# A five-layer float32 kernel on one core: loads issued before their use, and another order of steps in the latent layer

## The chip, the core and the metric

The kernel runs on one core of a Trainium2 chip. A core has TensorE (PE, matrix products and transposes), VectorE (DVE), ScalarE (ACT), GpSimd (POOL) and SyncE (SP, whose queue issues every load and store here). The metric is the device time of one execution in microseconds (us), lower is better; it is given as the median of several runs.

## The reference, cut to what matters

Two blocks of float32 layers work on 256 tokens of 2048 features. The first has a retention layer and a dilated attention layer, each with attention to 256 memory tokens; the second has a sliding-window layer (SWA) over the tokens and 256 context tokens, and a latent attention layer (MLA). Two facts matter below. Scales and shifts come from a small vector through a large matrix (`ada`):

```python
shift, scale, gate = jnp.split(cond @ ada_w[i] + ada_b[i], 3, axis=-1)
h = rmsnorm_2(x, norm_g[i]) * (1.0 + scale) + shift
```

And the latent layer normalises its keys before 16 heads attend:

```python
kv = (rmsnorm_2(c_kv, kva_g) @ w_kvb).reshape(B, S, H, MLA_NOPE + MLA_V)
k_nope = rmsnorm_2(kv[..., :MLA_NOPE], kn_nope_g)
s = (einsum('bqhd,bkhd->bhqk', qn, kn) + einsum('bqhr,bkr->bhqk', qp, kp)) * scale
p = softmax(s); o = einsum('bhqk,bkhd->bqhd', p, v)
```

## The kernel before

**Products.** Nearly all time goes into products of 256 or 512 tokens with weights. `gemm` (L191) walks over the weights in units of 1 MB: `wload` (L127) loads a unit into one of four `raw` tiles, ScalarE rounds it to the fast product type (`wh`, L134, three tiles), VectorE makes the remainder (`wl`, L135, two tiles), and TensorE forms activation high times `wh`, activation low times `wh`, and activation high times `wl`. Results add up in `acc`, of which there are five PSUM banks; `add_halves` (L300, L301) empties four banks into `mkT` pages: ScalarE copies one half, VectorE adds the other.

**Side work.** After each unit `gemm` calls `tick`, which moves every running generator (`spawn`, `later`) by one `yield`, and `fill(nfill)`, which takes a unit of `ada` from a list when its credit passes 1. An ada unit is a 1 MB load through the same four `raw` tiles and eight VectorE instructions (L383, L385); there are 96 of them. FA, FB and FS are the credits for one unit in the first, second and SWA part. 66 pages of 128x512 hold everything else. A scheduler then sets each engine's order by the order of the program and by what is free, so the order on an engine is near the written one but not the same.

**The places that the change touches.** (1) `mem_rows` and `enter_x` (L605, L616), run beside the memory keys (`mem_kv`, L629): they load `nat` (rows, summed in squares by ScalarE, `junk`) and `natT` pages (the transposed input, split into `ha`), and use each at once. (2) `enter_ctx` (L905), the same for the context, beside the out-product of the dilated layer. (3) The entry of SWA: the sums of L944 to L962 give `r23`, then `hT_mod` scales (`y`, L895) and transposes (`yT`) the input for the first product `kr` (L1019), whose first two units are taken for the context half before that (`ahead=2`). (4) `reload` (L1052): eight pages of attention results that were stored to DRAM (`mixsd`) come back as `mixSL` and are split by ScalarE into `mixSH` and by VectorE into `mixSL` (L325, L326), for SWA's out-product. (5) The latent layer: its first product (L1250), `kv_T` and `cq_T` (transposes of the latents), and then per pair of heads `mla_q` (L1336), `mla_kv` (L1382) and `mla_att` (L1408). A chain (two blocks of queries by two heads make four) has three stages: scores `ls` and softmax `lp`; transposes `pT` copied to `pTs`; products `lo` with the values and a gated write to `mixl`. `pipe` starts one chain in each of its steps and yields after every second step (MPER).

Of the kernel before, what the change touches and what calls it, by code (L numbers as in the profile page):

```python
# [22 lines left out]
S128 = 128 ** -0.5  # L23
NPAGES = 66
NRAW = 4
FA, FB, FS = 0.25, 0.23, 0.58
NMISC = 3
MPER = 2


class Act:
# [29 lines left out]
def tile_kernel(ctx: ExitStack, tc: tile.TileContext, d, out):  # L61
# [17 lines left out]
    def pg(s="pg", dt=F32, shape=None):  # L79
        return ppool.tile(shape or [P, 512], dt, name=nm(s), tag="pg")  # L80
# [506 lines left out]
        for k in range(2):  # L587
            split_gain(act, 2 * i + k, u[:, k * 256 : (k + 1) * 256], gain(gi, 2 * i + k))

    def enter(srcT, act, gi, c):  # L590
        for i in (2 * c, 2 * c + 1):
            enter_page(srcT, act, gi, i)

    def rows(src, q, c):
        for t in range(2):
            u = pg("nat")
            load(u, src[t * P : (t + 1) * P, c * 512 : (c + 1) * 512])
            sumsq(q[:, 4 * t + c : 4 * t + c + 1], u, 512)

    def row_rsqrt(dst, q):  # L600
        ssq = small(2)
# [2 lines left out]

    def mem_rows():  # L605
        q = const([P, 8], "ssm")
        for c in range(4):
            rows(d["mem"], q, c)
            yield
        row_rsqrt(memr, q)  # L610
        condition()
        yield
        bcast_rows(memrB[:, 0:256], memr)
        yield from enter_x()

    def enter_x():  # L616
        q = const([P, 8], "ssxa")
        for c in range(4):
            enter(d["xT"], ha, N_A, c)
            rows(d["x"], q, c)  # L620
            yield
        row_rsqrt(ra, q)
        V.tensor_scalar(sra, ra, 1.0 / 16.0, None, ALU.mult)
        V.tensor_scalar(hra, ra, 0.5, None, ALU.mult)
# [3 lines left out]
    def mem_kv(layer):  # L628
        kT, vn = [None] * 4, [[None] * 2 for _ in range(2)]  # L629
        w = d["w_mem_kv"][layer]  # L630
        if layer == 1:
            accs = gemm_wide(hm, w, 1024, [(0, 1), (1, 1)] + [(u, 2) for u in range(2, NK, 2)],
                             lambda u: u % 2 == 0 and enter_page(d["memT"], hm, MEM_N, u // 2))
            spawn(mem_rows())
            vs = [[pg("mkv") for _ in range(2)] for _ in range(2)]
            for c in range(2):
                for t in range(2):
                    A.copy(vs[c][t], accs[c][t])

            def post():  # L640
                for c in range(2):
                    for t in range(2):
                        A.activation(vs[c][t], vs[c][t], AF.Copy, scale=memr[:, t : t + 1])
                        load(memb[4 + 2 * t + c], vs[c][t])
            later(post, 7)
        for c in range(2):
            raw = add_halves(gemm_HL(hm, w, c * 512, FA if layer == 0 or c else 0), "mkT")

            def post(c=c, raw=raw):
                for j in range(2):  # L650
                    V.tensor_tensor(raw[j].rearrange("p (k n) -> p k n", k=2), raw[j].rearrange("p (k n) -> p k n", k=2),
                                    bc(memrB[:, 0:256], 2), ALU.mult)
                    if layer == 1:
                        load(memb[2 * c + j], raw[j])
                    else:
                        kT[2 * c + j] = split_page(raw[j], "mkTs")
            later(post, 5 if layer == 1 and c == 0 else 0)
        if layer == 0:
            for c in range(2):
                acs = gemm(hm, [0, 1], w, NK, 1024 + c * 512, nfill=FA)  # L660
                for t in range(2):
                    vn[t][c] = split_rows(acs[t], memr[:, t : t + 1])
        return kT, vn
# [240 lines left out]

    def enter_ctx():  # L905
        q, rc = const([P, 8], "ssc"), const([P, 2], "rc")
        for c in range(4):
            rows(d["ctx_2"], q, c)
        row_rsqrt(rc, q)
        yield  # L910
        rcB = pg("rcB")
        bcast_rows(rcB[:, 0:256], rc)
        for i in range(8):
            u = pg("natT")
            load(u, d["ctxT"][i])
            V.tensor_tensor(u.rearrange("p (k n) -> p k n", k=2), u.rearrange("p (k n) -> p k n", k=2),
                            bc(rcB[:, 0:256], 2), ALU.mult)
            split_mod(hs, 2 * i, 2, u, modA[0][:, 1, 2 * i : 2 * i + 2], adaT[0][:, 2 * i : 2 * i + 2, 1])
            if i % 2:
                yield  # L920

    def splitB(u):
        if u == 12:
# [88 lines left out]
    def evac4(acs):  # L1012
        res = [None] * 4
        for i, t in enumerate(TL):
# [1 line left out]
            A.copy(res[t], acs[i])  # L1016
        return res

    kr = evac4(gemm(hs, TL, WS, NK, 2048, nfill=FS,  # L1019
                    pre=lambda u: hT_mod([z[0][u // 4], z[1][u // 4]], r23, 0, 0, hs, u // 4), ahead=2))  # L1020
    kn = [None] * 4
    for t in TL:
# [27 lines left out]
            mixS.H[k], mixS.L[k] = pg("mixSH", F32R), pg("mixSL", F32R)  # L1050

    def reload():  # L1052
        for u in range(0, 8, 4):
            for k in range(u, u + 4):
                open_page(k)
                q = mixS.L[k].bitcast(F32)
                load(q, mixsd[k])
                split_in_place(mixS, k)
            yield

    for j in range(4):
        qr = evac4(gemm(hs, TL, WS, NK, j * 512, nfill=FS))
# [171 lines left out]
    def rope_pe(dst, src, rs, t, o, g):  # L1234
# [11 lines left out]
        for j in range(2):  # L1246
# [1 line left out]
        V.tensor_tensor(dst, dst, b, ALU.add)  # L1248

    acs = gemm(None, [(hl[1], 0), (hl[1], 1), (hl[0], 0), (hl[0], 1)], WL, NK, 512, 320,  # L1250
               pre=lambda u: hT_mod([x3[0][u // 4], x3[1][u // 4]], r3, 1, 0, hl[0], u // 4))
    ckv, kpq = [None] * 4, [None] * 4
    for i, t in enumerate(TL):
        ss, u, rs = small(2), small(2), small(2)
# [27 lines left out]
                tr(ps[:, t * P : (t + 1) * P], kpq[t][:, o : o + P])  # L1282
            A.copy(dst, ps)

    later(kv_T)
    acs = gemm(hl[0], [0, 1], WL, NK, 0, 512)
    cq = []
    for t in range(2):
# [14 lines left out]
            for k in range(2):  # L1303
                split_gain(hq, 2 * j + k, ps[:, k * 256 : (k + 1) * 256], gT[:, 6 * NK + 2 * j + k : 6 * NK + 2 * j + k + 1])

    later(cq_T)
    mixl = new_act(NK, 256, "mixl")
    S192 = 192 ** -0.5
    gsl = {}
# [19 lines left out]
    def mla_q(hp, r):  # L1329
        acs = gemm(hq, [0, 1], d["mla_w_qb_2"], 4, hp * 384, 384, mid=True)  # L1330
        qn = [pg("qn") for _ in range(2)]
        qp = [pg("qp", F32R) for _ in range(2)]
        ss8, rs8, evs = small(8), small(8), []
        for t in range(2):
            ev = pg("qev")
            A.copy(ev[:, 0:384], acs[t][:, 0:384])  # L1336
            v4 = ev[:, 0:384].rearrange("p (e w) -> p e w", e=2)
            sq = pg("sq")
            A.activation(sq[:, 0:384], ev[:, 0:384], AF.Square)
            s4 = sq[:, 0:384].rearrange("p (e w) -> p e w", e=2)  # L1340
            V.tensor_reduce(ss8[:, 2 * t : 2 * t + 2], s4[:, :, 0:P], AX, ALU.add)
            V.tensor_reduce(ss8[:, 4 + 2 * t : 6 + 2 * t], s4[:, :, P:192], AX, ALU.add)
            evs.append((ev, sq))
        V.tensor_scalar(ss8[:, 0:4], ss8[:, 0:4], 1.0 / P, EPS, ALU.mult, ALU.add)
        V.tensor_scalar(ss8[:, 4:8], ss8[:, 4:8], 1.0 / 64, EPS, ALU.mult, ALU.add)
        G.tensor_tensor(rs8, ss8, nhalf[:, :8], ALU.pow)

        def scale(t):
            ev, sq = evs[t]
            v4 = ev[:, 0:384].rearrange("p (e w) -> p e w", e=2)  # L1350
            pe = sq[:, 384:512].rearrange("p (e w) -> p e w", e=2)
            q3 = qp[t][:, 0:256].rearrange("p (e s w) -> p e s w", e=2, s=2)
            for e in range(2):
                V.scalar_tensor_tensor(qn[t][:, e * P : (e + 1) * P], v4[:, e, 0:P], rs8[:, 2 * t + e : 2 * t + e + 1],
                                       g_qk, ALU.mult, ALU.mult)
            rope_q(pe, v4[:, :, P:192], rs8[:, 4 + 2 * t : 6 + 2 * t], t)
            V.tensor_copy(q3[:, :, 0, :], pe)
            V.tensor_tensor(q3[:, :, 1, :], pe, q3[:, :, 0, :].bitcast(F32), ALU.subtract)

        def post():  # L1360
            for t in range(2):
                scale(t)
            for _ in range(2):
                yield
            ps = misc("qT")
            for e in range(2):
                for t in range(2):
                    tr(ps[:, e * 256 + t * P : e * 256 + (t + 1) * P], qn[t][:, e * P : (e + 1) * P])
            r["q"] = split_page(ps, "qT")
            ps = misc("qpT")  # L1370
            for e in range(2):
                for t in range(2):
                    tr(ps[:, e * 256 + t * P : e * 256 + (t + 1) * P], qp[t].bitcast(F32)[:, e * P : (e + 1) * P])
            r["qp"] = pg("qpT", F32R)
            A.copy(r["qp"], ps)
        spawn(post())

    def mla_kv(hp, r):
# [13 lines left out]
        rsqrt(rs8, ss8, P)  # L1392

        def post():
            for t in range(4):
                v4 = kv[t].rearrange("p (e s w) -> p e s w", e=2, s=2)
                for e in range(2):
                    A.activation(v4[:, e, 0, :], v4[:, e, 0, :], AF.Copy, scale=rs8[:, 2 * t + e : 2 * t + e + 1])
            for _ in range(2):
                yield  # L1400
            r["k"] = []
# [7 lines left out]
    def mla_att(hp, r):  # L1409
# [34 lines left out]
            return [st0, st1, st2]  # L1444

        def attend():
            for _ in range(4):
                yield
            yield from pipe([chain(t, e) for t in range(2) for e in range(2)], MPER)
            mix_out(mix, mixl, hp)  # L1450

        spawn(attend())
# [116 lines left out]
```

## Time and profile before

| | us |
|---|---|
| median of 3 runs | 3096.49 (3095.86 to 3096.86) |
| the profiled execution | 3096.07 |
| its span, first to last instruction | 3094.3 |
| TensorE / VectorE / ScalarE / GpSimd busy | 3042.5 / 2163.8 / 1411.2 / 86.2 |
| mean granted TensorE clock, share of full speed | 0.995 |

The span is what the trace covers; 1.8 us of the execution's time lie around it. TensorE is busy 98% of the span, so the views to read are those of its waits and of the clock granted to it; a row of waits names the instruction that waited, and the one that released it.

### The profile page before, as it was taken

To read this page: it belongs to the slowest core of one execution; us is meant where nothing else is said; L and a number is where in the kernel's file an instruction comes from. 1 tells how busy PE (TensorE), PEld (TensorE's weight loads), DVE (VectorE), ACT (ScalarE), POOL (GpSimd) and SP (SyncE) were. 2 spreads that over 40 slices of the span, in tenths; PEclk is the share of its full clock that TensorE was granted. 3 is DMA by queue.
4 is the path that set the end of the run, shared out by engine and by line. 5 is a ranking of instruction groups with operands and counts; after the bars stand their busy time and mean duration, and the time that the engine had idled before them with its cause. 6 is when DMAs were issued, how large, how long until landed. Compare 5 with 4: busy or idle time off the path is not lost.

```text
span 3094.3 us, 38864 instructions
## 1 busy us (share of the span) xinstructions
PE 3042.5 (98%) x15386; PEld 2570.2 (83%) x15386; DVE 2163.8 (70%) x3277; ACT 1411.2 (46%) x1870; POOL 86.2 (3%) x63
## 2 busy tenths in 40 slices
PE   9799999999999999999999999999999999999999
PEld 7688888888888888888888888788888778888887
DVE  5677877878867767766766747867676766656774
ACT  6444444445433433433433555424355342645662
POOL 0000000000000000000000000010110100000110
PEclk9899999999999999999999999999999999999999
DMA  8776676677566656656656667544433435453234
GB/s 307 242 243 226 210 245 222 221 260 264 206 208 234 232 185 227 222 195 227 231 191 227 222 224 248 181 157 156 136 118 108 163 103 180 145 176 123 69 103 129
DMA packets 307863, 600.77 MB, mean 194 GB/s; under 512 B 12896, under 2 KB 24800, under 8 KB 307680
## 3 DMA queue, kind: packets, MB, share of 16 engines
q1 hardware_dynamic: 307680, 598.29, 57.3%
q8 instruction: 120, 1.97, 0.3%
q14 instruction: 63, 0.52, 0.0%
HBM read 585.62 MB, written 12.62 MB: 193 GB/s over the span
## 4 chain that ended last, share of the span: by engine, by line
PE 92%; DVE 4%; DMA 1%; ACT 1%; POOL 1%; issue 1%; SPq 0%; DVEq 0%; ACTq 0%
PE acc L99 83%; PE pT L111 2%; PE so L99 1%; PE bs L99 1%; PE ls L99 1%; PE bo L99 1%; DMA raw<-in_ada_w 1%; DVE wl L135 1%; PE xs L99 1%; DVE ada L385 1%; PE lo L99 1%; PE mixT L111 0%; PE mo L99 0%; PE ms L99 0%; PE yT L111 0%
## 5 line engine op out<-in xcount | busy, mean ns | idle before, releaser
L135 DVE TENSOR_TENSOR wl<-raw,wh 128x2048 fp32r<-128x2048 f32 (+2 forms) x437 | 982.2, 2248 | 601.8 <-PE acc L99 343.4
L134 ACT CAST wh<-raw 128x2048 fp32r<-128x2048 f32 (+2 forms) x437 | 821.0, 1879 | 1136.3 <-PE acc L99 1021.0
L385 DVE SCALAR_TENSOR_TENSOR ada<-raw,condth,ada 128x512 f32<-128x512 f32 x720 | 496.0, 745 | 60.7 <-DMA raw<-in_ada_w 60.5
L99 PE MATMUL acc<-hb,wh 128*128 128x512 f32 x896 | 232.6, 393 | 0.0
L99 PE MATMUL acc<-wh,ha 128*128 128x512 f32 x896 | 215.2, 392 | 0.0
L99 PE MATMUL acc<-hk,wh 128*128 128x512 f32 x768 | 199.4, 394 | 0.1
L99 PEld LDWEIGHTS acc<-wh,ha 128*128 128x128 f32 x896 | 166.3, 188 | 33.5
L99 PE MATMUL acc<-wh,hk 128*128 128x512 f32 x768 | 185.3, 393 | 0.0
L99 PEld LDWEIGHTS acc<-hb,wh 128*128 128x128 f32 x896 | 159.8, 188 | 27.0 <-DVE hb L443 0.5
L99 PEld LDWEIGHTS acc<-wh,hk 128*128 128x128 f32 x768 | 143.1, 188 | 28.6
L99 PEld LDWEIGHTS acc<-hk,wh 128*128 128x128 f32 x768 | 136.7, 188 | 22.5 <-DVE bq L301 0.4
L99 PE MATMUL acc<-wh,hsH 128*128 128x512 f32 x384 | 151.2, 397 | 0.0
L99 PE MATMUL acc<-wh,hsL 128*128 128x512 f32 x384 | 150.6, 395 | 0.0
L99 PEld LDWEIGHTS acc<-hb,wl 128*128 128x128 f32 x896 | 126.1, 190 | 11.8 <-ACT hb L442 0.2
L99 PE MATMUL acc<-hb,wl 128*128 128x256 f32 x896 | 129.8, 282 | 0.0
L99 PEld LDWEIGHTS acc<-hk,wl 128*128 128x128 f32 x768 | 108.0, 190 | 10.2
L99 PE MATMUL acc<-hk,wl 128*128 128x256 f32 x768 | 110.9, 282 | 0.0
L99 PE MATMUL acc<-wl,ha 128*128 128x512 f32 x448 | 110.7, 389 | 0.0
L99 PE MATMUL acc<-wh,mixSH 128*128 128x512 f32 x256 | 101.2, 400 | 5.8 <-ACT mixSH L325 3.8
L99 PE MATMUL acc<-wh,mixSL 128*128 128x512 f32 x256 | 101.0, 400 | 2.2 <-DVE mixSL L326 2.2
L99 PE MATMUL acc<-hsH,wh 128*128 128x512 f32 x256 | 99.7, 391 | 0.0
L99 PE MATMUL acc<-hsL,wh 128*128 128x512 f32 x256 | 99.3, 390 | 0.0
(404 smaller groups left out, 5405.1 us busy)
## 6 DMA issues: line engine op xcount, KB each, us to landing
raw<-in_ada_w SPq DMA_DIRECT2D x96, 1024.0 KB, 5.1
raw<-in_w_kv SPq DMA_DIRECT2D x96, 1024.0 KB, 5.0
raw<-in_w_in_b SPq DMA_DIRECT2D x80, 1024.0 KB, 5.0
raw<-in_w_in_a SPq DMA_DIRECT2D x64, 1024.0 KB, 5.3
raw<-in_swa_w_in SPq DMA_DIRECT2D x40, 1024.0 KB, 5.0
raw<-in_w_mem_kv SPq DMA_DIRECT2D x31, 1024.0 KB, 5.3
raw<-in_w_out_a SPq DMA_DIRECT2D x24, 1024.0 KB, 5.2
raw<-in_w_out_b SPq DMA_DIRECT2D x24, 1024.0 KB, 5.2
```

What stands on the lines that cost most here:

```text
L99: T.matmul(o, lhsT=l, rhs=r, start=start, stop=stop)
L111: T.transpose(o, i, ident[:k, :k])
L134: A.copy(h, rw)
L135: V.tensor_tensor(l, rw, h.bitcast(F32), ALU.subtract)
L385: V.scalar_tensor_tensor(a[ci], raw[:, k, :], col, a[ci], ALU.mult, ALU.add)
```

## The change

What it does, part by part. A helper `staged(n, begin, end, lag)` issues the loads of step i and uses those of step i-lag, one step a tick. `mem_rows` and `enter_x` run by it with a lag of 2, `enter_ctx` with a lag of 1 for rows and 2 for pages (one page a tick, before two), `reload` with two steps of four pages and a lag of 1. The `later` waits in `mem_kv` go from 7 to 8 and from 5 and 0 to 6 and 3. The `kr` product has no `nfill` (its four units give no ada credit), and FS goes from 0.58 to 0.64, so 44 units give 28.2 credits where 48 gave 27.8. The first product of the latent layer gets `ahead=2`. `kv_T` and `cq_T` come one tick later. The keys are scaled by 32 VectorE products of 128x2x128 in place of 64 ScalarE instructions of 128x128. `mla_q` and `mla_kv` yield once ahead of their scaling. `attend` waits five ticks in place of four and runs pairs of chains (the two heads of one block), one stage a tick, older pairs first.

```diff
-FA, FB, FS = 0.25, 0.23, 0.58
+FA, FB, FS = 0.25, 0.23, 0.64
-MPER = 2
...
+    def staged(n, begin, end, lag=2):
+        got = []
+        for i in range(n + lag):
+            if i < n:
+                got.append(begin(i))
+            if i >= lag:
+                end(i - lag, got[i - lag])
+            yield
...
     def mem_rows():
         q = const([P, 8], "ssm")
-        for c in range(4):
-            rows(d["mem"], q, c)
-            yield
+        yield from staged(4, lambda c: load_rows(d["mem"], c), lambda c, us: sum_rows(q, c, us))
...
     def enter_x():
-        for c in range(4):
-            enter(d["xT"], ha, N_A, c)
-            rows(d["x"], q, c)
-            yield
+        def begin(c):
+            return [load_page(d["xT"][i]) for i in (2 * c, 2 * c + 1)], load_rows(d["x"], c)
+        def end(c, got):
+            for i in range(2):
+                for k in range(2):
+                    split_gain(ha, 4 * c + 2 * i + k, got[0][i][:, k * 256 : (k + 1) * 256], gain(N_A, 4 * c + 2 * i + k))
+            sum_rows(q, c, got[1])
+        yield from staged(4, begin, end)
...
-            later(post, 7)
+            later(post, 8)
...
-            later(post, 5 if layer == 1 and c == 0 else 0)
+            later(post, (6, 3)[c] if layer == 1 else 0)
...
     def enter_ctx():
-        for c in range(4):
-            rows(d["ctx_2"], q, c)
+        yield from staged(4, lambda c: load_rows(d["ctx_2"], c), lambda c, us: sum_rows(q, c, us), 1)
...
+        yield from staged(8, lambda i: load_page(d["ctxT"][i]), end)
...
-    kr = evac4(gemm(hs, TL, WS, NK, 2048, nfill=FS,
+    kr = evac4(gemm(hs, TL, WS, NK, 2048,
                     pre=lambda u: hT_mod([z[0][u // 4], z[1][u // 4]], r23, 0, 0, hs, u // 4), ahead=2))
...
     def reload():
-        for u in range(0, 8, 4):
-            for k in range(u, u + 4):
+        def begin(i):
+            for k in range(4 * i, 4 * i + 4):
                 open_page(k)
-                q = mixS.L[k].bitcast(F32)
-                load(q, mixsd[k])
+                load(mixS.L[k].bitcast(F32), mixsd[k])
+        def end(i, _):
+            for k in range(4 * i, 4 * i + 4):
                 split_in_place(mixS, k)
-            yield
+        yield from staged(2, begin, end, 1)
...
-               pre=lambda u: hT_mod([x3[0][u // 4], x3[1][u // 4]], r3, 1, 0, hl[0], u // 4))
+               pre=lambda u: hT_mod([x3[0][u // 4], x3[1][u // 4]], r3, 1, 0, hl[0], u // 4), ahead=2)
...
-    later(kv_T)
+    later(kv_T, 1)
...
-    later(cq_T)
+    later(cq_T, 1)
...
         def post():
+            yield
             for t in range(2):
                 scale(t)
...
         def post():
+            yield
             for t in range(4):
-                v4 = kv[t].rearrange("p (e s w) -> p e s w", e=2, s=2)
-                for e in range(2):
-                    A.activation(v4[:, e, 0, :], v4[:, e, 0, :], AF.Copy, scale=rs8[:, 2 * t + e : 2 * t + e + 1])
+                k3 = kv[t].rearrange("p (e s w) -> p e s w", e=2, s=2)[:, :, 0, :]
+                V.tensor_tensor(k3, k3, rs8[:, 2 * t : 2 * t + 2].unsqueeze(2).to_broadcast([P, 2, P]), ALU.mult)
...
         def attend():
-            for _ in range(4):
+            for _ in range(5):
                 yield
-            yield from pipe([chain(t, e) for t in range(2) for e in range(2)], MPER)
+            pairs = [[chain(t, e) for e in range(2)] for t in range(2)]
+            for i in range(len(pairs) + 2):
+                for j in (2, 1, 0):
+                    if 0 <= i - j < len(pairs):
+                        for c in pairs[i - j]:
+                            c[j]()
+                yield
             mix_out(mix, mixl, hp)
```

Three places show how it moves instructions. Rows of the changed kernel carry its own line numbers. The first place is ScalarE beside the memory keys: `ha` and `junk` wait for loads of x, `mkT` empties the four PSUM banks of a finished product, `wh` prepares weights. Before:

```order
L123 ACTIVATE junk_815,ssxa<-nat_813 128x512
L123 ACTIVATE junk_819,ssxa<-nat_817 128x512
L319 ACTIVATE ha_129<-natT_859,gT 128x256
L319 ACTIVATE ha_130<-natT_859,gT 128x256
L319 ACTIVATE ha_131<-natT_865,gT 128x256
L319 ACTIVATE ha_132<-natT_865,gT 128x256
L300 COPY mkT_899<-acc_645 128x256
L300 COPY mkT_899<-acc_646 128x256
L300 COPY mkT_904<-acc_647 128x256
L300 COPY mkT_904<-acc_648 128x256
```

After, from the copy that ends the row scales `memrB`:

```order
L133 CAST wh_966<-raw_965 128x2048
L571 COPY memrB_137<-rB_815 128x256
L299 COPY mkT_839<-acc_637 128x256
L299 COPY mkT_839<-acc_638 128x256
L299 COPY mkT_844<-acc_639 128x256
L299 COPY mkT_844<-acc_640 128x256
L122 ACTIVATE junk_961,ssxa<-nat_823 128x512
L122 ACTIVATE junk_963,ssxa<-nat_824 128x512
L122 ACTIVATE junk_1019,ssxa<-nat_895 128x512
L133 CAST wh_1028<-raw_1027 128x2048
```

The copies of `mkT` stood behind six pages of `ha` and four of `junk`; they now stand ahead of all of them.

The second is SP at the end of SWA's last heads, where `mixSL` pages come back and `raw` carries weights and ada units. Before:

```order
L96 DMA raw_19593<-in_ada_w 128x4x512
L96 DMA mixSL_18981<-mixsd 128x512
L96 DMA mixSL_18986<-mixsd 128x512
L96 DMA raw_19603<-in_swa_w_out 128x4x512
L96 DMA mixSL_18991<-mixsd 128x512
L96 DMA raw_19765<-in_ada_w 128x4x512
L96 DMA mixSL_18996<-mixsd 128x512
L96 DMA raw_19828<-in_swa_w_out 128x4x512
L96 DMA mixSL_19055<-mixsd 128x512
L96 DMA raw_19914<-in_swa_w_out 128x4x512
```

After:

```order
L95 DMA raw_19593<-in_ada_w 128x4x512
L95 DMA mixSL_18967<-mixsd 128x512
L95 DMA mixSL_18970<-mixsd 128x512
L95 DMA mixSL_18973<-mixsd 128x512
L95 DMA mixSL_18976<-mixsd 128x512
L95 DMA mixSL_19033<-mixsd 128x512
L95 DMA mixSL_19036<-mixsd 128x512
L95 DMA mixSL_19039<-mixsd 128x512
L95 DMA mixSL_19042<-mixsd 128x512
L95 DMA raw_19603<-in_swa_w_out 128x4x512
```

The eight pages stood between five `raw` loads; they now follow one another behind a single one.

The third is TensorE in the latent attention, from the end of one chain's scores; `acc<-wl` rows belong to the product that runs beside it. Before:

```order
L99 MATMUL ls_22692<-kpHH_21285,qpT_22264 128x512
L99 MATMUL ls_22692<-kpLL_21286,qpT_22264 128x512
L111 MATMUL pT_22706<-ident,lp_22647 128x128 x4
L99 MATMUL lo_22713<-kv_22418,pTs_22658 128x128
L99 MATMUL lo_22713<-kv_22420,pTs_22658 128x128
L99 MATMUL lo_22713<-kv_22422,pTs_22658 128x128
L99 MATMUL lo_22713<-kv_22424,pTs_22658 128x128
L99 MATMUL acc_22769<-wl_22773,hkvH_21281 128x512
L99 MATMUL acc_22767<-wl_22773,hkvH_21282 128x512
L99 MATMUL ls_22719<-kT_22543,qT_22255 128x512
L99 MATMUL ls_22719<-kT_22543,qT_22256 128x512
L99 MATMUL ls_22719<-kT_22544,qT_22255 128x512
```

After:

```order
L98 MATMUL ls_22734<-kpHH_21285,qpT_22283 128x512
L98 MATMUL ls_22734<-kpLL_21286,qpT_22283 128x512
L98 MATMUL acc_22694<-wl_22700,hkvH_21281 128x512
L98 MATMUL acc_22695<-wl_22700,hkvH_21281 128x512
L98 MATMUL ls_22748<-kT_22543,qT_22274 128x512
L98 MATMUL ls_22748<-kT_22543,qT_22275 128x512
L98 MATMUL ls_22748<-kT_22544,qT_22274 128x512
L98 MATMUL ls_22748<-kpHH_21285,qpT_22283 128x512
L98 MATMUL ls_22748<-kpLL_21286,qpT_22283 128x512
L98 MATMUL acc_22696<-wl_22700,hkvH_21281 128x512
L98 MATMUL acc_22697<-wl_22700,hkvH_21281 128x512
L98 MATMUL acc_22694<-wl_22700,hkvH_21282 128x512
```

The transposes `pT` and products `lo` of the pair before stood right behind the scores; now the scores of both heads come first with eight rows of the running product around them (the last three are cut here), and `lo` and `pT` behind these.

On PE, SP and GpSimd the instructions are otherwise the same ones in number. VectorE has 32 scalings more and 15 copies of `pTs` fewer; ScalarE has 64 scalings fewer and these 15 copies more. At the entry of the latent layer the order on TensorE is the same in both kernels.

## Rows read from the trace of the kernel before

**Rows 1.** The page: busy us of an engine, share, instructions.

```profile
PE 3042.5 (98%) x15386; PEld 2570.2 (83%) x15386; DVE 2163.8 (70%) x3277; ACT 1411.2 (46%) x1870; POOL 86.2 (3%) x63
```

**Rows 2.** Waits of TensorE, whole span: total us, times, longest.

```profile
PE acc L99 <- DVE mkT L301: 16.6, 1, 16.6
PE acc L99 <- ACT wh L134: 7.1, 1, 7.1
PE acc L99 <- ACT mixSH L325: 3.8, 1, 3.8
PE yT L111 <- ACT y L895: 3.7, 2, 3.4
PE pT L111 <- ACT qpT L1375: 3.6, 3, 1.6
PE acc L99 <- DVE mixSL L326: 2.2, 2, 1.4
PE acc L99 <- ACT mixSH L316: 1.8, 1, 1.8
PE mixT L111 <- DVE mixl L1442: 1.2, 3, 0.7
PE acc L99 <- DVE hlH L339: 1.1, 1, 1.1
PE rB L99 <- DVE dg L569: 1.0, 1, 1.0
...
PE kvT L111 <- ACT ckv L1261: 0.7, 1, 0.7
...
PE kpT L111 <- DVE kpq L1265: 0.6, 1, 0.6
```

**Rows 3.** Busy time by window; the clock column (after POOL) is 0.50 throughout.

```profile
106.16:123.23 17.07, 4.75 (x14) 4.00 (x15) 7.27 (x17) 9.40 (x26) 0.00 (x0) 0.50 0.70 236
1939.12:1942.53 3.41, 2.88 (x11) 2.59 (x12) 2.83 (x6) 1.75 (x4) 0.00 (x0) 0.50 0.57 216
2461.36:2468.19 6.83, 5.34 (x12) 3.74 (x13) 6.83 (x14) 2.38 (x7) 0.00 (x0) 0.50 0.04 16
```

**Rows 4.** Timeline at 100 us: start, length, instruction, [idle before it <- releaser].

```profile
100.83 1.09 PE L99 MATMUL acc<-hm,wh 128*128 128x512 f32 x4
...
95.29 0.38 SPq L96 DMA_DIRECT2D raw<-in_ada_w  x1
...
112.63 0.91 ACT L319 ACTIVATE ha<-natT,gT 128x256 fp32r<-128x256 f32 x2 [4.07 <-DMA natT<-in_xT]
...
117.39 1.16 ACT L300 COPY mkT<-acc 128x256 f32<-128x256 f32 x4
...
101.28 5.38 DVE L385 SCALAR_TENSOR_TENSOR ada<-raw,condth,ada 128x512 f32<-128x512 f32 x8
...
117.92 1.41 DVE L301 TENSOR_TENSOR mkT<-acc,mkT 128x256 f32<-128x256 f32 x4
119.25 1.28 DVE L651 TENSOR_TENSOR mkT<-mkT,memrB 128x512 f32<-128x512 f32 x2
```

**Rows 5.** Timeline of VectorE ahead of the entry of SWA.

```profile
1924.60 3.40 DVE L385 SCALAR_TENSOR_TENSOR ada<-raw,condth,ada 128x512 f32<-128x512 f32 x5 [2.56 <-DMA raw<-in_ada_w]
...
1931.92 2.07 DVE L385 SCALAR_TENSOR_TENSOR ada<-raw,condth,ada 128x512 f32<-128x512 f32 x3
```

**Rows 6.** The key scaling (L1398): its time each, and what ScalarE awaited before it.

```profile
L1398 ACT ACTIVATE kv<-kv,sm x64: 385/392/406, 2809.4 to 2993.2; 128x128 f32<-128x128 f32 x64
...
  POOL sm L119: 13.4, 8
```

**Rows 7.** Groups by form: a VectorE product of 128x256, and the copies of pTs.

```profile
L301 DVE TENSOR_TENSOR bk<-acc,bk 128x256 f32<-128x256 f32 x48 | 20.0, 420 | 11.8 <-ACT bk L300 11.8
...
L499 DVE COPY pTs<-pT x27: 670/681/693, 1088.0 to 3015.8; 128x512 f32<-128x512 f32 x27
```

**Rows 8.** Busy time in the latent attention, columns as in rows 3.

```profile
2900.00:2950.00 50.00, 46.91 (x285) 40.05 (x285) 39.13 (x128) 34.24 (x79) 9.56 (x4) 1.00 0.22 74
```

More of the change, by code (lines that the diff above doesn't have):

```diff
@@ L588, in enter_page, with load_rows, sum_rows, load_page @@
             split_gain(act, 2 * i + k, u[:, k * 256 : (k + 1) * 256], gain(gi, 2 * i + k))
[L590 to L594, printed above, removed]
-        for t in range(2):
-            u = pg("nat")
-            load(u, src[t * P : (t + 1) * P, c * 512 : (c + 1) * 512])
-            sumsq(q[:, 4 * t + c : 4 * t + c + 1], u, 512)
+    def staged(n, begin, end, lag=2):
[6 more added lines that the diff above has]
+            yield
+    def load_rows(src, c):
+        us = [pg("nat") for _ in range(2)]
+        for t in range(2):
+            load(us[t], src[t * P : (t + 1) * P, c * 512 : (c + 1) * 512])
+        return us
+    def sum_rows(q, c, us):
+        for t in range(2):
+            sumsq(q[:, 4 * t + c : 4 * t + c + 1], us[t], 512)
+    def load_page(src):
+        u = pg("natT")
+        load(u, src)
+        return u
     def row_rsqrt(dst, q):
@@ L912, in enter_ctx, with end @@
         bcast_rows(rcB[:, 0:256], rc)
-        for i in range(8):
-            u = pg("natT")
-            load(u, d["ctxT"][i])
+        def end(i, u):
             V.tensor_tensor(u.rearrange("p (k n) -> p k n", k=2), u.rearrange("p (k n) -> p k n", k=2),
@@ L918, in enter_ctx @@
             split_mod(hs, 2 * i, 2, u, modA[0][:, 1, 2 * i : 2 * i + 2], adaT[0][:, 2 * i : 2 * i + 2, 1])
-            if i % 2:
-                yield
+        yield from staged(8, lambda i: load_page(d["ctxT"][i]), end)
     def splitB(u):
@@ L1052, in reload @@
     def reload():
-        for u in range(0, 8, 4):
-            for k in range(u, u + 4):
+        def begin(i):
+            for k in range(4 * i, 4 * i + 4):
                 open_page(k)
-                q = mixS.L[k].bitcast(F32)
-                load(q, mixsd[k])
+                load(mixS.L[k].bitcast(F32), mixsd[k])
+        def end(i, _):
+            for k in range(4 * i, 4 * i + 4):
                 split_in_place(mixS, k)
-            yield
+        yield from staged(2, begin, end, 1)
     for j in range(4):
```

## The prediction

> **What bounds the kernel now.** I read the page first: TensorE is busy 3042.5 of 3094.3 us [rows 1], so 51.8 us of the span are without a product, and no edit takes a product away. The change can give back idle time, time at half clock, and what hides between products; nothing else. Then TensorE's waits [rows 2]: the reader is to see that they are few, one place each, and which engine released each. At the start 7.1 us go before the first weights are ready; the end is the last stores; neither is touched. The longest wait is 16.6 us for the additions into mkT, once, at the entry. Then come reload (mixSH 3.8, mixSL 2.2), the transposes yT at the entry of SWA (3.7, of which 3.4 in one wait), pT, mixT and the latents' kvT and kpT in the latent layer (3.6, 1.2, 0.7, 0.6), rB of the context (1.0). Last I read the granted clock by window: at three of these places it stood at 0.50 of full speed, 1.2 GHz in place of 2.4, after TensorE had stood still [rows 3].
>
> What half clock costs is read from TensorE's busy time there: half of what it did in these windows would have been saved. In the first window that is half of 4.75, 2.4 us; in the second half of 2.88, 1.4; in the third half of 5.34, 2.7; together 6.5. The idle part of the windows is already in the waits.
>
> By a term in the Trainium skill (TensorE: Matmul & The Clock Gate, section Terms), the loss is about the throttled time times the missing share of the clock, here half of 27.3 us [rows 3] or 13.7 us. The rows disagree, since only 13.0 us of these 27.3 were busy; with the page's figure the sum below would be 41.8 instead of 34.6, and the time 3054.
>
> **Entry.** ScalarE waited for loads of x, 4.07 us for the last before its split [rows 4], and the four copies of mkT, 1.16 us, stood in the queue behind that until 117.39; VectorE's additions followed at 117.92, 1.41 us for four, and each frees a PSUM bank. TensorE had run out of banks at 100.83 + 1.09 = 101.9 [rows 4]. In the changed order these copies stand ahead of everything that needs x, so the 16.6 goes. What is late next: VectorE has one ada instruction, two multiplications and two more ada instructions ahead of the first addition: 3 x 0.67 (5.38 over 8) + 1.28 + 0.35 = 3.6 us [rows 4], and the first waits for its raw tile. Before, a raw of that kind went out at 95.29 and was in use at 101.28; SP reaches the one of the changed order at about the same place among the weights. If it lands by 98.3 nothing is left of the wait; if only at 101.28, 3.0 us are; if it goes out one weight unit later, about 8. I take 2.5, near the middle of the first two, because the ada raw is issued ahead of all x loads. The 12 x loads now stand behind it on SP, and behind them two stores of mkT, which wait for the multiplication, and only then the third unit of the next product; two units already loaded cover this, and where they do not, it is part of the 8. The wait of 2.5 is short against the 16.6 after which the clock fell, so I also count the 2.4. Gain 16.6 + 2.4 - 2.5 = 16.5, between 9 and 19.
>
> **Context and entry of SWA.** The wait for rB, 1.0, goes: many more products stand ahead of it when pages come one a tick; between 0 and 1.3. At the entry of SWA the chain from the additions to y was held by eight ada instructions on VectorE, five ahead (3.40 us) and three inside (2.07), with their transposes and reductions between the small steps [rows 5]. With kr without nfill the changed order has no ada instruction from the additions to r23. That is 5.5 us off a chain that came 3.4 us late, so y is early, and next late is nothing on TensorE, which has the two context units. Gain 3.4 + 1.4 of clock = 4.8, between 2 and 4.9. The ada units that kr no longer takes are spread by FS 0.64 over the heads: each is a load on SP and eight instructions, 5.38 us on VectorE. One now falls ahead of the rotation of the last heads' queries, with TensorE's transposes behind it; I take 0.5 lost, between 0 (hidden by TensorE's next products) and 4.
>
> **Reload.** Each mixSL load stood behind a raw load that waits for its tile; the pages came one by one. Eight now follow behind one ada raw, ScalarE splits them in a row, and the weight split behind them is not needed until TensorE reaches the second unit. The three waits (3.8 + 2.2) and 2.7 of clock go: 8.7, between 3 (the pages' old users free them late and SP stands) and 9. The 1.8 for mixSH of the last heads [rows 2] stays, since that order hardly changes.
>
> **Latent layer.** The entry with ahead=2 gives nothing: the order on TensorE is the same before and after, and the 1.1 for hlH [rows 2] stays. kv_T one tick later lets kvT and kpT stop waiting: 0.7 + 0.6 = 1.3, between 0 and 2. In the attention, pT and mixT waited 3.6 + 1.2 [rows 2], because transposes stood close behind the scores whose softmax they need; with products of the neighbour gemm between, these 4.8 go. The last head pair has nothing beside it: three steps of the drain stay open, each with a copy of pTs, 0.68 [rows 7], so I give back 2.0. Net 2.8. The key scaling takes 64 x 392 = 25.1 us from ScalarE [rows 6] and puts 32 on VectorE; no row shows 128x2x128 with a broadcast factor, so I bound it by the 420 ns of a 128x256 product and the 681 of a 128x512 copy [rows 7], and take 420 for the like number of elements: 13.4 us, against 15 copies fewer, 10.2. VectorE is then 3 us busier over the eight pairs, and it was at 39.13 of 50 us [rows 8], so beside TensorE this costs nothing; if the cover is gone, see the rival. Between -14 and +8.
>
> **Sum.** 16.5 + 1.0 + 4.8 - 0.5 + 8.7 + 1.3 + 2.8 = 34.6. Against the profiled execution's 3096.1 (span 3094.3 and 1.8 around it, 0.4 under the median, which is less than what is open here): 3061.5, forecast 3061. A measurement of this kernel can tell about 0.2%, 6 us, from no change.
>
> **Rivals.**
> (a) The stall at the entry only moves. TensorE's first bank still waits for VectorE, now behind ada instructions that wait for a raw; with x loads also in flight that raw, or the third unit of the next product, lands late. If half of 16.6 stays with the half clock, 8.3 + 2.4 come back: 3072. For it: three ada instructions still stand ahead of the additions. Against: copies and additions need no x any more. 15%.
> (b) VectorE becomes late in the latent attention. ScalarE stood 13.4 us, eight times, in front of the key scaling for POOL's reciprocal root [rows 6]. If VectorE now stands there instead, softmax, weight remainders and copies queue behind it: 13.4 + 13.4 - 10.2 = 16.6 on the path and the 2.8 lost: 3081. For it: VectorE is the second busiest engine [rows 1]. Against: post now yields once before it scales, and VectorE has 11 of 50 us free [rows 8]. 12%.
> (c) More than the waits show comes back. A break between two products that is shorter than the modelled end of a product is in no row; the latent attention has 32 chains of three stages. If as much again as the 4.8 hides there, the drain costs nothing and the entry leaves nothing, 4.8 + 2.0 + 2.5: 3052; with all ends of the terms about 3046. 10%.
> (d) Slower: loads ahead hold up SP's one queue. A load waits there for its page, and the weight loads stand behind it. Three groups are issued ahead (x, context, mixS). If each holds the weights as long as the longest wait seen, 16.6, that is 49.8: 3111. It decides from (34.6 + 6.2) / 3 = 13.6 us a group. Against: weights have four raw tiles, and the reload pages waited mostly for raw loads ahead of them, not the reverse. 3%.
> (e) The change does not do what it says, as at the latent entry: the scheduler had the order already, 3096. The orders shown speak against it at three places. 3%.
>
> **How the numbers follow.** The forecast, within 3053 to 3070, has 57%; (a) 15, (b) 12, (c) 10, (d) 3, (e) 3. The range 3046 to 3079 holds the forecast, (a) and (c), 82%; (b) lies just over it. Faster by over 0.2%: the forecast and (a) to (c), 94%; within 0.2%: (e), 3%; slower: (d), 3%.
>
> **What would show it.** Right: in the waits of TensorE the mkT row is at most 5 us, mixSH L324 and mixSL are gone, yT is under 0.5, pT and mixT together under 2.5; the clock does not stand at 0.50 at 106, 1939 or 2461. Wrong: a wait for mkT or wh over 8 us near 105 (a); waits for kT, pT or wl in the last 250 us over 10 us, with VectorE idle for POOL (b); SP waiting for pages with raw loads behind it (d).

## The result and the profile after

The changed kernel takes 3062.24 us (3059.77 to 3064.26, 4 runs) against 3096.68 (3095.86 to 3097.73): a ratio of 0.9888, interval 0.9871 to 0.9905. The forecast was 3061, within 3046 to 3079. The profiled execution is the fastest of the four, with a span of 3058.0, so its span is 36.3 us shorter.

TensorE's waits over the whole span, as in [rows 2] (total, times, longest):

```profile
PE acc L98 <- ACT wh L133: 6.8, 2, 6.5
PE acc L98 <- DVE mkT L300: 1.7, 1, 1.7
PE acc L98 <- DVE hlH L338: 1.1, 1, 1.1
PE qT L110 <- DVE mixlL L486: 1.0, 1, 1.0
PE pT L110 <- DVE pTs L455: 1.0, 2, 0.8
PE acc L98 <- DVE hsH L338: 0.9, 1, 0.9
PE xs L98 <- DVE pTs L455: 0.8, 1, 0.8
...
PE acc L98 <- ACT mixSH L315: 0.5, 1, 0.5
PE ls L98 <- DVE kT L455: 0.5, 1, 0.5
PE pT L110 <- ACT lp L1449: 0.4, 1, 0.4
```

The 16.6 for mkT is 1.7; the waits for yT, the reloaded mixSH and mixSL, rB, kvT and kpT are gone from the head of the list. Nothing over 1.7 is left but the start. The page's busy times after:

```profile
PE 3033.5 (99%) x15386; PEld 2564.6 (84%) x15386; DVE 2160.6 (71%) x3294; ACT 1401.2 (46%) x1821; POOL 81.8 (3%) x63
```

The same windows of the places that stood at half clock (columns as in [rows 3]; the places come earlier now) show 1.00:

```profile
101.00:105.00 4.00, 2.34 (x13) 1.85 (x12) 4.00 (x10) 1.46 (x5) 0.00 (x0) 1.00 1.02 357
1915.00:1919.00 4.00, 3.69 (x21) 2.80 (x19) 3.76 (x6) 2.78 (x6) 0.00 (x0) 1.00 0.15 54
2425.00:2432.00 7.00, 6.64 (x29) 4.98 (x28) 4.60 (x6) 2.47 (x5) 0.00 (x0) 1.00 0.62 206
```

The kernel before had a fourth stretch at half clock that [rows 3] do not list, behind the wait of 1.8 us for mixSH in the last heads:

```profile
2515.97:2519.38 3.41, 3.41 (x15) 3.02 (x15) 0.67 (x2) 2.04 (x4) 0.00 (x0) 0.50 0.01 2
```

In the changed kernel it is gone too. TensorE's busy time fell by 9.0 us for the same products (3042.5 to 3033.5); half of its busy time in the four stretches is 8.2.

TensorE executes the same number of products in both kernels, so places can be compared by number: the table gives the time between the starts of the nth and the mth product, us, from the trace of each kernel (the names of the experiments are told below).

| products | place | before | after | entry alone | kr alone | reload alone | latent alone |
|---|---|---|---|---|---|---|---|
| 0 to 600 | entry | 136.2 | 119.1 | 118.8 | 135.5 | 136.3 | 135.6 |
| 8500 to 9600 | context | 217.8 | 216.6 | 217.8 | 217.8 | 217.8 | 217.8 |
| 9600 to 9960 | entry of SWA | 84.4 | 80.6 | 84.2 | 80.3 | 86.3 | 86.0 |
| 9960 to 12000 | SWA heads | 435.1 | 434.3 | 435.4 | 435.0 | 435.2 | 435.9 |
| 12000 to 12400 | reload | 94.7 | 86.2 | 94.7 | 94.0 | 85.9 | 94.0 |
| 12400 to 12700 | last heads | 68.4 | 68.5 | 68.4 | 66.9 | 66.6 | 68.1 |
| 13300 to 13700 | kvT, kpT, cqT | 80.9 | 79.4 | 80.9 | 80.9 | 80.9 | 79.3 |
| 13900 to 15200 | latent attention | 237.7 | 234.8 | 236.7 | 237.9 | 238.0 | 234.9 |

Places left out agree within 0.8 us. At the entry VectorE, ScalarE and TensorE now read (timeline: start, length, instruction, [idle before it <- releaser]):

```profile
96.94 2.29 DVE L134 TENSOR_TENSOR wl<-raw,wh 128x2048 fp32r<-128x2048 f32 x1 [3.08 <-PE acc L98]
...
99.19 1.20 ACT L299 COPY mkT<-acc 128x256 f32<-128x256 f32 x4
...
99.15 0.74 DVE L384 SCALAR_TENSOR_TENSOR ada<-raw,condth,ada 128x512 f32<-128x512 f32 x1
99.82 1.28 DVE L669 TENSOR_TENSOR mkT<-mkT,memrB 128x512 f32<-128x512 f32 x2
101.02 1.41 DVE L384 SCALAR_TENSOR_TENSOR ada<-raw,condth,ada 128x512 f32<-128x512 f32 x2
102.35 1.41 DVE L300 TENSOR_TENSOR mkT<-acc,mkT 128x256 f32<-128x256 f32 x4
...
102.91 1.17 PE L98 MATMUL acc<-hm,wh 128*128 128x512 f32 x4 [1.66 <-DVE mkT L300]
```

The copies come at 99.19 in place of 117.39 [rows 4]. The additions stand behind three ada instructions and two multiplications, as counted; the first ada instruction follows the weight split `wl` without a gap, and its raw landed at 99.03.

### The profile page after: what moved, and what is told of

It is laid out like the page before. It is cut to its first block, busy times and chain, and to the rows that moved or that the text cites. A ratio compares the mean times of both kernels' runs of the same rounds, so it can differ in the third digit from the quotient of the medians.

```text
span 3058.0 us, 38825 instructions
## 1 busy us (share of the span) xinstructions
PE 3033.5 (99%) x15386; PEld 2564.6 (84%) x15386; DVE 2160.6 (71%) x3294; ACT 1401.2 (46%) x1821; POOL 81.8 (3%) x63
## 4 chain that ended last, share of the span: by engine, by line
PE 92%; DVE 4%; DMA 1%; POOL 1%; ACT 1%; issue 0%; SPq 0%; POOLq 0%; DVEq 0%
PE acc L98 83%; PE pT L110 1%; DVE wl L134 1%; DMA raw<-in_ada_w 1%; PE bs L98 1%; PE bo L98 1%; PE so L98 1%; DVE ada L384 1%; PE lo L98 1%; PE xs L98 1%; PE ls L98 1%; PE mixT L110 0%; PE mo L98 0%; PE ms L98 0%; PE cs L98 0%
## 5 line engine op out<-in xcount | busy, mean ns | idle before, releaser
L98 PEld LDWEIGHTS acc<-hk,wl 128*128 128x128 f32 x768 | 108.0, 190 | 10.1
```

The source lines that it names most:

```text
L98: T.matmul(o, lhsT=l, rhs=r, start=start, stop=stop)
```

## Experiments

### One part at a time, on the kernel before

**Entry alone** (`b1_entry`): `mem_rows`, `enter_x` and the later waits as in the changed kernel, nothing else.

> The kernel before with one part alone: mem_rows and enter_x staged (lag 2) and the later waits 8, 6, 3. Theory (the gains are separate, each at its place): the wait of 16.6 us for mkT shrinks to about 1.7 as in the changed kernel, the stretch at half clock near 106 us is gone, and the rest of the kernel keeps its waits (yT 3.4, mixSH 3.8, mixSL 2.2, pT 3.6): 16.5 to 17.5 us faster than before, near 3079.5. Rival (the places are coupled, a kernel that arrives earlier at one place waits more at the next because loads keep their pace): part of the gain is eaten later, under 13 us faster, and the waits at SWA or reload grow.

**kr alone** (`b2_kr`):

```diff
-FA, FB, FS = 0.25, 0.23, 0.58
+FA, FB, FS = 0.25, 0.23, 0.64
-    kr = evac4(gemm(hs, TL, WS, NK, 2048, nfill=FS,
+    kr = evac4(gemm(hs, TL, WS, NK, 2048,
```

> The kernel before with one part alone: the kr product takes no ada units, FS 0.64. Theory: the wait of yT (3.4) and the half clock near 1939 go, 3.5 to 5 us faster, near 3092; the reload keeps its waits of 3.8 and 2.2 since its loads still stand between weight loads. Rival (the ada units in the heads decide the reload too, since they take raw tiles and a place on SP ahead of mixSL): the mixSH and mixSL waits change by over 2 us as well, in either direction, and the gain is not 3.5 to 5.

**Reload alone** (`b3_reload`): `reload` by `staged(2, begin, end, 1)`.

> The kernel before with one part alone: reload staged in two steps of four pages with a lag of 1. Theory: eight mixSL loads follow one another on SP, the waits for mixSH (L325, 3.8) and mixSL (2.2) and the half clock near 2461 go: 8 to 9 us faster, near 3088. The wait at 2515 of 1.8 and its half clock stay, if they belong to the last heads; rival: they are a consequence of the late reload, since all that follows was pushed into one another, and go too, 10 to 12 us faster.

**Latent alone** (`b4_latent`): all edits from the first latent product on.

> The kernel before with one part alone: everything from the first latent product on as in the changed kernel (ahead=2, kv_T and cq_T a tick later, yields, keys scaled on VectorE, pairs of chains). Theory: kvT and kpT no longer wait (1.3), pT, mixT and kT wait 2 to 3 in place of 5.5: 4 to 5.5 us faster, near 3092; VectorE waits for the reciprocal root of GpSimd ahead of the scaling by about 8 us in all, and TensorE does not notice. Rival (the latent gain comes from what stands ahead of it, ada units or the SWA tail, not from this part): under 2 us faster.

Measured, beside 3096.26 for the kernel before: 3079.21, 3089.51, 3087.41 and 3092.49, so 17.1, 6.8, 8.9 and 3.8 us less; ratios 0.9948 (0.9932 to 0.9965), 0.9980 (0.9971 to 0.9989), 0.9971 (0.9961 to 0.9982), 0.9988 (0.9979 to 0.9997). The sum is 36.6, and with the 1.2 of the context, which was not run alone, 37.8; the whole change gave 34.4, and 36.9 when it was run again (3061.11 beside 3098.04). So the gains are separate, nearly all at their places, as the table shows; the entry's early arrival is not eaten later.

Entry and reload came within what their theories gave. kr alone gave 6.8 for at most 5: beside the 4.1 at the entry of SWA, with the ada units elsewhere the last heads lose their wait of 1.8 for mixSH (now 0.5) and their half clock, and that stretch takes 66.9 for 68.4. The reload's waits, from the waits of TensorE with kr alone, stay nearly as they were:

```profile
PE acc L99 <- ACT mixSH L325: 3.5, 1, 3.5
PE acc L99 <- DVE mixSL L326: 1.7, 2, 1.1
```

The reload alone does the same to the last heads (66.6; mixSH waits 1.0, and the half clock is gone), so at this place its rival was nearer, though the whole stayed within the theory's 8 to 9. Both together do not (68.5 in the changed kernel): waits for pTs, 1.0 and 0.8 above, come in their place.

Latent alone gave 3.8 for at least 4: its own places give 4.4 in the table (80.9 to 79.3, 237.7 to 234.9), but the entry of SWA, where nothing was edited, took 1.6 longer. The wait for yT there differs between kernels that all leave that place as it was: 3.0 us in its one long wait with the entry alone, 3.4 before, 4.2 and 4.8 with reload and latent alone. VectorE's timeline tells why; here it is with the entry alone and with the latent part alone:

```profile
1906.52 3.41 DVE L385 SCALAR_TENSOR_TENSOR ada<-raw,condth,ada 128x512 f32<-128x512 f32 x5 [2.08 <-DMA raw<-in_ada_w]
```

```profile
1925.16 3.40 DVE L385 SCALAR_TENSOR_TENSOR ada<-raw,condth,ada 128x512 f32<-128x512 f32 x5 [3.94 <-DMA raw<-in_ada_w]
1928.48 1.28 DVE L944 TENSOR_TENSOR x1r<-acc,x1r 128x512 f32<-128x512 f32 x2
```

VectorE stood 2.08, 2.56 [rows 5], 3.35 (reload alone) and 3.94 us for the load of the ada unit, with the additions queued behind it, and yT waited 3.0, 3.4, 4.2 and 4.8: 0.9 more each time. The chain was held by that load as well as by the five instructions.

### The entry: what stands ahead of the copies, and what is left

**Lag 0** (`a4_lag0`), on the changed kernel:

```diff
-        yield from staged(4, begin, end)
+        yield from staged(4, begin, end, 0)
```

> The changed kernel with enter_x staged with lag 0: loads of x and their use in one tick again, the rest as changed. The copies of mkT now stand behind four ha and one junk instruction on ScalarE, and the additions behind four ha and four ada instructions on VectorE. Theory (what counts is what waits for x ahead of the copies): TensorE waits 4 to 9 us for mkT, 2.5 to 8 us slower than the changed kernel, 3065 to 3070. Rival (the later waits for the row scales and stores, 8, 6 and 3, made the gain at the entry): the wait stays at 1.7 and the time at 3062.

**One ada unit later** (`a5_ada_later`), on the changed kernel:

```diff
-        raw = add_halves(gemm_HL(hm, w, c * 512, FA if layer == 0 or c else 0), "mkT")
+        raw = add_halves(gemm_HL(hm, w, c * 512, (2 * FA if layer == 0 else FA) if c else 0), "mkT")
```

> The changed kernel with one ada unit taken later: none in the first product of the second mkT pair, two in the next. On VectorE the three ada instructions ahead of the additions are gone. Theory (what is left of the wait at the entry, 1.7 us, is these three instructions, 2.15 us): the wait for mkT is 0 to 0.3, and the time 1.2 to 1.9 us under the changed kernel, 3060 to 3061. Rival (the third unit of the next product, behind x loads on SP, would be waited for instead, or the two ada units later collide with ha): the wait moves to wh or ha and the time stays or grows by up to 5.

Lag 0 measured 3064.97 (3063.85 to 3066.43). That is 2.7 and 3.9 over the changed kernel's two medians. TensorE waits 3.9 us for mkT, just under the 4 expected, and starts at half clock after it: four products take 2.05 us, where they took 1.17 after the wait of 1.66. The clock stands at 0.50 from 104.14 to 110.97 us, with TensorE busy for 4.86 of it.

```profile
106.11 2.05 PE L98 MATMUL acc<-hm,wh 128*128 128x512 f32 x4 [3.90 <-DVE mkT L300]
...
103.30 1.67 DVE L319 SCALAR_TENSOR_TENSOR ha<-natT,gT,ha 128x256 fp32r<-128x256 f32 x4
104.88 0.74 DVE L384 SCALAR_TENSOR_TENSOR ada<-raw,condth,ada 128x512 f32<-128x512 f32 x1
105.54 0.42 DVE L300 TENSOR_TENSOR mkT<-acc,mkT 128x256 f32<-128x256 f32 x1
```

So the lag is worth 4.6 us of the entry (123.7 for 119.1 us in products 0 to 600), by what stands ahead of the additions: 2.2 us of wait and half of 4.86, 2.4, of clock. The other 12.5 of the gain remain with lag 0, hence come from the rest of that part. One effect of it is in the order: `mem_rows` with its lag ends two ticks later, so `enter_x` starts later, and with lag 0 four ha and one junk instruction stand between memrB and the first copy of mkT, where twelve and four did in the kernel before. What the later waits give by themselves was not run.

The ada unit later measured 3059.17 (3058.39 to 3060.69); the wait for mkT is gone from the list, products 0 to 600 take 117.6, and the third weight unit is not waited for. Without the three ada instructions nothing was left of the wait. The version is 0.9876 of the kernel before (0.9861 to 0.9891), 2 to 3 us under the changed kernel's two medians and the lowest median here; the intervals of the whole times overlap (0.9871 to 0.9905 for the changed kernel), so the gain is read from the stretch, 117.6 and, in the run with four ticks below, 117.9, where seven traces with the lag and without this edit have 118.8 to 119.9.

### The latent attention: parts that do not add

On the changed kernel, the key scaling back on ScalarE (`a1_scale_act`):

```diff
-                V.tensor_tensor(k3, k3, rs8[:, 2 * t : 2 * t + 2].unsqueeze(2).to_broadcast([P, 2, P]), ALU.mult)
+                for e in range(2):
+                    A.activation(v4[:, e, 0, :], v4[:, e, 0, :], AF.Copy, scale=rs8[:, 2 * t + e : 2 * t + e + 1])
```

> The changed kernel with the key scaling put back on ScalarE (64 instructions of 128x128), all else as changed. Theory (the latent gain comes from pairs and yields, the scaling lies beside TensorE on either engine): within 1.5 us of the changed kernel, 3061 to 3064, VectorE some 10 us less busy there, ScalarE some 20 more, the waits for kT and pT together within 1 us of before the edit. Rival (the scaling on ScalarE blocks copies and softmax behind GpSimd's reciprocal root): 3 to 6 us slower than the changed kernel, with waits for kT or qT of over 2 us.

The chains run as before (`a2_old_attend`): `attend` of the kernel before, with `pipe` and four ticks.

> The changed kernel with the attention chains run as before (one chain started per step, two steps a tick, four ticks ahead), the scaling on VectorE and the yields kept. Theory: the waits for pT and mixT come back, 3 to 5 us, and the kernel is 2.5 to 4.5 us slower than the changed one, 3065 to 3067. Rival (the yields ahead of the scaling made the gain): within 1 us of the changed kernel.

Beside the changed kernel once more (`after_again`): no yields (`a7_no_yield`: both added `yield` lines out), both undone (`a8_old_act`: the edits of the two runs above), and four ticks (`a10_attend4`: `range(5)` in `attend` to `range(4)`, with the ada unit later).

> The changed kernel itself once more, beside the next three on the same chip, since its own runs lie 4.5 us apart: 3059 to 3065 by either theory.

> The changed kernel without the two yields ahead of the scaling in mla_q and mla_kv. Theory (the engine that scales stands still for GpSimd's reciprocal root, and what hurts is what stands in its queue behind it; the yield moves the scaling back so that the root is ready): VectorE waits more for GpSimd ahead of the scaling than the 8.5 us of the changed kernel, 12 or more, and the latent attention (TensorE from product 13900 to 15200 in its order) takes 2 to 5 us longer than 234.8. Rival (the yields only move the order, VectorE has time for the wait): 234 to 236 us, the same time as the changed kernel.

> The changed kernel with both parts of the latent attention undone and only the yields kept: keys scaled on ScalarE and chains run as before. This is the fourth corner: pairs with VectorE gave 234.8 us for the latent attention, old chains with VectorE 238.1, pairs with ScalarE 242.6. Theory (pairs put two softmaxes behind one blocked scaling on ScalarE, old chains only one): 236.5 to 238.5 us, as in the kernel before (237.7), so the place of the scaling is worth nothing with old chains and 7.8 with pairs. Rival (ScalarE's scaling is bad with any order, and the kernel before was saved by having no yields): over 240 us.

> The changed kernel with the ada unit later at the entry (as in the run before) and the attention starting after four ticks in place of five. The first edit should give again what it gave: no wait for mkT, 1.2 to 1.9 us under the changed kernel of this call. For the second: by the theory that scores wait for keys and queries made ready by VectorE, a tick less brings waits of ls for kT or qT, 2 to 6 us more in the latent attention; rival (the fifth tick is only distance, and lengthens the drain): 0 to 2 us less there.

| chains | scaling | yields | ticks | products 13900 to 15200 | TensorE's waits there | stand for GpSimd's root | kernel, median |
|---|---|---|---|---|---|---|---|
| old | ScalarE | no | 4 | 237.7 (before) | 5.5 | 13.4 | 3096.68 |
| old | ScalarE | yes | 4 | 236.2 | 5.2 | 7.1 | 3063.05 |
| old | VectorE | yes | 4 | 238.1 | 6.2 | 3.0 | 3063.75 |
| pairs | ScalarE | yes | 5 | 242.6 | 10.1 | 18.2 | 3069.59 |
| pairs | VectorE | no | 5 | 246.0 | 10.8 | 12.8 | 3073.70 |
| pairs | VectorE | yes | 4 | 242.6 | 9.2 | 7.1 | 3067.22 (ada unit later) |
| pairs | VectorE | yes | 5 | 234.8 and 234.9 (changed, twice) | 2.9 | 8.5 | 3062.24, 3061.11 |

The first row differs from the others in every other part of the change as well, so its median is not to be compared with theirs, only its stretch. TensorE's waits are those that its rows list from 2750 us on; the stand is that of the engine that scales, ahead of its scaling. Old chains with five ticks, pairs on ScalarE without the yields and old chains on VectorE without them were not run.

Five executions with the latent part of the changed kernel lie between 234.8 and 234.9 in this stretch; four with that of the kernel before between 236.7 and 238.0, so there a difference counts from about 1.5. Pairs of chains are slower than the kernel before in three of four forms, by 5 to 8 us; only with the scaling on VectorE, the yields and the fifth tick are they faster, by 2 to 3. The yields with the old chains give 0.5 to 1.8, which is hardly clear of that spread. For the scaling on ScalarE the rival was right, and went further than expected (7.4 and 8.5 us by the medians). For the old chains the kernel was expected at 3065 to 3067 and came at 3063.75, 1.5 to 2.6 over the changed one: a miss. Its stretch is 3.3 us longer, but in the slowest of its four runs; mixT waits 4.0 as the theory said, pT does not wait, and one stand of 2.2 us for kT is followed by half clock from 2833.1 to 2836.5, with TensorE busy all of these 3.4 us:

```profile
PE ls L98 <- DVE kT L455: 2.2, 1, 2.2
```

For the yields the theory was right, with a size above its own. With four ticks the stretch is longer, as the theory said and by more, but ls waits only 1.0 for kT; the other waits are not those that it named. For the fourth corner its number was a little high.

What the rows show of the cause, first on ScalarE's timeline with pairs and its own scaling:

```profile
2883.40 1.57 ACT L1417 ACTIVATE kv<-kv,sm 128x128 f32<-128x128 f32 x5 [2.63 <-POOL sm L118]
2884.88 0.67 ACT L1450 ACTIVATE lp<-ls,sm 128x512 f32<-128x512 f32 x1
2885.45 0.19 ACT L1450 ACTIVATION_READ_ACCUMULATOR lp<-ls,sm 128x1 f32 x1
2885.54 0.39 ACT L1417 ACTIVATE kv<-kv,sm 128x128 f32<-128x128 f32 x1
2885.83 0.67 ACT L1450 ACTIVATE lp<-ls,sm 128x512 f32<-128x512 f32 x1
```

ScalarE stands for GpSimd's root, then scales, and both heads' softmaxes (lp) are queued behind; TensorE waits behind these. The waits of ScalarE and of TensorE there:

```profile
ACT kv L1417 <- POOL sm L118: 18.2, 8, 3.2
```

```profile
PE qpT L110 <- ACT lp L1450: 4.5, 4, 1.2
```

On VectorE the same wait is 8.5 us over the eight pairs in the changed kernel and 12.8 without the yields (from VectorE's waits in both):

```profile
DVE kv L1416 <- POOL sm L118: 8.5, 8, 1.8
```

```profile
DVE kv L1414 <- POOL sm L118: 12.8, 8, 1.8
```

Without the yields TensorE's transposes and scores wait for both engines, 3.3 for pT and 2.0 for ls among them. With four ticks it is pT, lo and kT, 2.0 each:

```profile
PE pT L110 <- ACT lp L1449: 2.0, 3, 1.1
PE lo L98 <- ACT lp L1449: 2.0, 4, 0.5
PE kT L110 <- DVE mixl L1460: 2.0, 4, 0.7
```

The old chains with the yields and the scaling on ScalarE have one sort of wait left:

```profile
PE mixT L110 <- DVE mixl L1461: 5.2, 5, 1.4
```

The stretch follows TensorE's waits in the table: in order of the one, the rows are in order of the other but for the two at 242.6. Against the changed kernel the waits give 7.2 of 7.8 us for the scaling on ScalarE, 6.3 of 7.7 for the fifth tick and 7.9 of 11.2 for the yields; what the rest of these is was not resolved. The stand for GpSimd's root does not order the stretches: with four ticks it is 7.1, less than the 8.5 of the changed kernel, and the stretch is 7.7 longer. So that stand, with the softmax behind it, is shown for pairs with the scaling on ScalarE; for the yields it is one part (4.3 us more), and why the fifth tick matters is not shown beyond the waits above.

## Why the prediction was right

**Entry**, 16.5 forecast, 17.1 measured. The remaining wait was 1.7 for the 2.5 taken. The raw landed at 99.03, 0.7 after the 98.3 at which nothing would have been left; but VectorE was in the weight split `wl` until 99.2 as well, which the chain had left out, so an earlier landing would have given nothing. TensorE ran out of banks at 101.25, not 101.9, as the start was 0.6 shorter. The run with the ada unit later shows that the three instructions were the remainder. The half clock went, as counted: 14.9 less wait and 2.4 of clock are 17.3. Rival (a)'s price counted the 2.5 twice; half of 16.6 with the half clock would have been 3070, not 3072. That only the copies' place behind x made the stall is more than the runs show: lag 0 puts part of x back ahead of them and brings back 4.6 us, not 16.6.

**Context**, 1.0, measured 1.2. **Entry of SWA**, 4.8, measured 3.8. The term that was mis-sized is "next late is nothing": hsH is late next, by 0.9, and 3.4 + 1.4 - 0.9 are 3.9. What ada held up was not all counted either, though the wait for yT went all the same: I took 5.5 us off the chain, from eight instructions, but the additions had also waited for the landing of an ada load, 2.56, and in the changed kernel other waits fill part of the room, here on VectorE:

```profile
1911.45 0.69 DVE L961 TENSOR_TENSOR x1r<-x1r,gf 128x512 f32<-128x512 f32 x1 [1.55 <-ACT junk L122]
...
1914.61 0.16 DVE L977 TENSOR_TENSOR r<-r 128x2 f32<-128x2 f32 x1 [1.12 <-POOL r L976]
```

**SWA heads**, -0.5: nothing was lost (434.3 for 435.1; the stretch varies between 434.1 and 435.9).

**Reload**, 8.7, measured 8.5: SP issues the eight loads in one row, 5.03 us, and ScalarE splits them in one, as the order said.

```profile
2401.85 5.03 SPq L95 DMA_DIRECT2D mixSL<-mixsd  x8
...
2407.21 5.38 ACT L324 CAST mixSH<-mixSL 128x512 fp32r<-128x512 f32 x8 [1.96 <-DMA mixSL<-mixsd]
```

The wait of 1.8 for the last heads did not stay, as I had written, and its half clock went too; but other waits, 1.8 for pTs among them, came in that stretch, so that the nothing which I had counted for it came out by luck (68.5 for 68.4). **kvT and kpT**, 1.3, measured 1.5. `ahead=2` at the latent entry gave nothing, 125.5 us for products 12700 to 13300 against 125.4.

**Latent attention**, 2.8, measured 2.9: right in size, by luck, and wrong in cause. The step that failed is that pairs would remove 4.8 by themselves and the scaling cost nothing beside TensorE. In the waits, pT and mixT went from 4.8 to 1.1 and kT's 0.7 went, but qT, ls and lo now wait 1.8; that is 2.6 of the 2.9, and the 2.0 that I gave back for the drain stands in no row. With pairs the scaling's place is worth 7.8 us (242.6 for 234.8), the fifth tick 7.7 and the yields 11.2, and each of them is needed for pairs to gain at all. With old chains no difference between the engines is shown: 238.1 for 236.2, but 1.7 of that is the half clock above, and the medians are 0.7 apart. The price of the scaling was right (32 products of 418 ns, 13.4 us). Rival (b) named an engine that stands for GpSimd's root with the softmax behind it; the runs show that on ScalarE with pairs (18.2 us), and with all three edits together it did not decide on VectorE (8.5 us, with 2.9 of waits on TensorE).

**The sum.** In the two traces the places give 36.3 for the 34.6: 1.3 more at the SWA heads, 0.6 each at the entry and the start, 1.0 less at the entry of SWA, the others within 0.2. The medians, 34.4 apart, lie nearer to the forecast than the parts do; the start (7.1, then 6.5) and the heads vary by as much from run to run, so the closeness is partly luck.

By the page's figure in the Trainium skill (TensorE: Matmul & The Clock Gate, Terms) the whole would have been 41.8 and 3054, an estimate. The runs do not agree: the clock's three windows all went, and the gain was 34.4. At the entry, with 14.9 less wait, half of the busy time of the window makes 17.3 and half of its length 23.4; 17.1 was measured.

## What to carry to other kernels

Where one engine is busy 98% of the time, list its waits, add half of its busy time in the windows at half clock, and price each edit by the place where its wait ends last: those gains added up here to within 4 us of the whole (37.8 for 34.4). Where several edits meet in one pipelined stage they need not add, and a sum that comes out does not show the cause: run the edits one by one and in combination, and read every engine's order for an instruction that waits for another engine, and for what stands behind it. At the entry the loads issued ahead paid by what no longer stood behind their use.

## What was not expected of the hardware

The landing of the same load, ahead of the entry of SWA, varied between kernels that do not change that place: 10.1 to 11.5 us from its issue. VectorE stood 2.08 to 3.94 us for it, and TensorE's wait for yT moved by the same 1.8. At the entry TensorE came back at half clock, 1.2 GHz, after a stand of 3.9 us, and at full clock after one of 1.66, so the 2.2 us of wait that the lag removes there cost another 2.4. Two values do not show how long a stand it takes: in the kernel before half clock followed the stand of 1.83 at 2515, and in the run with the old chains one of 2.23.
